# Weight sums of the projection behind the merge: made by accumulating DMAs in DRAM instead of by VectorE

## The chip, the cores and the metric

The kernel runs on one core of a Trainium2 chip. The metric is the device time of one execution in microseconds, the median of several runs. All inputs lie in the device's DRAM at the start, the output lies there at the end. The engines of the core are TensorE (PE in the profile), VectorE (DVE), ScalarE (ACT), GpSimd (POOL) and SyncE (SP); each works through its own queue in order, and waits for the others through semaphores. Transfers are issued from the queues of SP, ACT and POOL.

## The reference, cut to what matters

One layer of a streaming encoder: 512 frames, 1024 features, float32. After a norm, one projection gives q, k, v, the inputs of a recurrence and two gates; attention and recurrence are projected (`ya`, `yb`), gated and merged; the merge goes through `w_o`, and a gated feed-forward block follows.

```python
xn = rmsnorm(h, norm_mix_g[l])
u = jnp.einsum('bsd,de->bse', xn, w_in[l])
q, k, v, xr, gr, ga, gb = jnp.split(u, splits, axis=-1)
ya = chunked_band_attention(q, k, v, rel_table[l]) @ w_attn_out[l]
xc = causal_depthwise_conv(xr, conv_w[l], conv_b[l])
hr = rg_lru(xc, w_rg_r[l], b_rg_r[l], w_rg_i[l], b_rg_i[l], rg_lambda[l])
yb = (hr * jax.nn.gelu(gr)) @ w_rnn_out[l]
g_a, g_b = jnp.split(jax.nn.sigmoid(jnp.concatenate([ga, gb], axis=-1) + b_merge[l]), 2, axis=-1)
h = h + (g_a * ya + g_b * yb) @ w_o[l]
gu = rmsnorm(h, norm_ffn_g[l]) @ w_ffn_in[l]
g, up = jnp.split(gu, 2, axis=-1)
h = h + (jax.nn.silu(g) * up) @ w_ffn_out[l]
return rmsnorm(h, final_norm_g)
```

`w_o` is 1024x1024, `w_ffn_in` 1024x5632, `w_ffn_out` 2816x1024. The change concerns the product with `w_o`.

## The kernel before

**Products in parts.** Every weight tile is split into a high part in a reduced format (ScalarE, L86) and the rest (VectorE, L87), and every product is three matmuls, high by high, high by low, low by high (`mm3`, L78 to L82). A tile of weights for one product is two pieces of 128x1024; each goes from DRAM into one of three buffers tagged `raw`, is split into a buffer tagged `whl`, and frees the raw buffer with its split. `prefetch` and `weights` (L416 to L454) make the tiles in the order of a list of names, so many names ahead of the product that asks.

**Products in blocks.** The products of `v`, of `w_o` (called `o`) and most of the feed-forward input (units fg0, fu0, fg1, fu1, fg2, fu2) and output are made by Winograd's form of Strassen's scheme: both factors are cut into 2x2 blocks, and seven block products of sums take the place of eight. With weight blocks b11, b12, b21, b22 the sums are t1 to t4; the products are named w11, w21, t1, t2, w22, t3, t4. The sums of the left factor for `o` are made from the merged rows `ta` in the loop at L1174 to L1192.

**Where the sums of weights come from.** For `v` and the later units VectorE makes them next to the product. For `o` and for fg0 (called `f`) they are made early, in the loop of the recurrence, by `sums_kept` (L321): it loads four blocks of one half (u = 0 or 1) into the pool `obp`, makes the four sums (L327 to L330), stores them to DRAM, and for those in `kept_parts` splits them and stores both parts (L337 to L340). It is called at the end of loop steps j = 2, 4, 6 for (`o`, 0), (`o`, 1), (`f`, 0) and after the first tiles of q and k for (`f`, 1). `kept_weights` (L344) loads them back: t1 and t2 of `o` are split then, t3 and t4 come as parts, straight into weight tiles. The pool is closed after the last call, and `aw`, `aw2`, the pools of the attention, are opened on its place; their tiles wait for the last use of what lay there.

For the feed-forward output VectorE makes no sums: `out_copy` (L222) copies a block within DRAM through SP's queue, and `out_add` (L226) adds another block onto it by an accumulating DMA through POOL's queue. There are 16 copies and 16 adds of 512 KB. One copy goes with each head of the attention; four adds go in heads 9, 11, 13, 15, four with the loop at L1174, eight in units fg1 and fg2.

**The order.** The attention is a loop over 16 heads: transposes of the probabilities of head h, one piece of other projection work (`fill`), the scores of head h + 2, and the product with v; before it, while `yb` is projected, the sums of x for `v` (`x_sums`, L966) and the sums of v's weights. TensorE's order is written out by hand from the `v` products on. Elsewhere a planner orders each engine's instructions by priority and by simulated readiness; `keep_in_program_order` pins an instruction behind the one written before it on the same engine. So the first of each of the sums of x is pinned behind what VectorE has to do for the keys of the second pair, and the copies and adds are pinned in SP's and POOL's queues. In the `o` product the order is w11, w21, t1, t2, w22, t3, then the first half of the norm, with t4 (L1251) between its transposes, then fg0's w11.

## Time and profile before

| | |
|---|---|
| Time, median of 3 runs | 847.2 us (847.09 to 848.59) |
| The profiled execution | 848.82 us, span 847.0 us |
| PE busy | 837.2 us (99%) |
| DVE busy | 654.1 us (77%) |
| ACT busy | 524.3 us (62%) |
| POOL busy | 159.9 us (19%) |
| DMA | 153.96 MB, mean 182 GB/s |
| granted clock | 0.997 |

The busy time of PE counts a matmul from its start to its modelled end, and matmuls overlap: one of 512 columns is shown with some 0.39 us while the next starts 0.23 us after it. So a late matmul shows in the distance of starts, and only a longer stall as idle time. In rows of a group the columns are the line, the engine, the operation, out<-in, the count, and durations in ns; in rows of a timeline the start and the duration in us come first, and in brackets stands the idle time before the instruction with what ended it. In a table of stretches the columns are the stretch, its length, busy us of PE, PEld, DVE, ACT and POOL with their instructions, the granted clock, the DMA share and GB/s.

### The profile page before, as it was taken

Reading aid. Unit: us, or ns where it says so; the run is one execution under the profiler, and the core shown is the slowest. Engines: PE = TensorE matmul, PEld = TensorE weight load, DVE = VectorE, ACT = ScalarE, POOL = GpSimd, SP = SyncE. Lnnn points to the kernel's source line nnn. Section 1 sums busy time; section 2 is a strip of 40 time slices with the busy share of each in tenths; the row PEclk is TensorE's granted clock in tenths of the full one; section 3 lists DMA queues with packets and bytes.
Section 4 is the critical chain, followed back from the end, with each engine's and each line's share of the span. In section 5 each row is a group of like instructions: output and inputs, shape, how many; then the busy total and the mean of one; then the engine's idle time right before and its main releaser. Section 6 shows DMA issues by size and latency. Waiting matters only on the chain.

```text
span 847.0 us, 11664 instructions
## 1 busy us (share of the span) xinstructions
PE 837.2 (99%) x4102; PEld 708.8 (84%) x4102; DVE 654.1 (77%) x960; ACT 524.3 (62%) x868; POOL 159.9 (19%) x207
## 2 busy tenths in 40 slices
PE   9999999999999999999999999999999999999996
PEld 6988888888878888888888888888888999988885
DVE  6667779886999778777568777889777878599784
ACT  7595848773456678878544469663765466555543
POOL 2412030221040043343211000005102322200000
PEclk9999999999999999999999999999999999999998
DMA  8433386687565444549448984555955576455442
GB/s 286 166 103 117 130 298 243 212 271 243 167 205 150 132 134 148 157 152 223 94 132 211 320 294 154 157 187 166 229 176 159 150 187 207 140 177 168 160 165 99
DMA packets 104058, 153.96 MB, mean 182 GB/s; under 512 B 8024, under 2 KB 62896, under 8 KB 103488
## 3 DMA queue, kind: packets, MB, share of 16 engines
q1 hardware_dynamic: 99040, 141.32, 51.2%
q0 software_dynamic: 3728, 8.96, 6.4%
q10 hardware_dynamic: 1232, 2.95, 0.9%
q8 instruction: 32, 0.52, 0.3%
q14 instruction: 26, 0.21, 0.1%
HBM read 139.53 MB, written 30.45 MB: 201 GB/s over the span
## 4 chain that ended last, share of the span: by engine, by line
PE 84%; DVE 7%; ACT 4%; DMA 3%; issue 2%; ACTq 0%; DVEq 0%
PE fu_x L80 2%; PE fu_x L81 2%; PE fu_x L82 2%; PE o L1122 2%; PE fg_x L82 2%; PE fg_x L80 2%; PE fg_x L81 2%; PE pT L1102 2%; PE po_ga L82 2%; PE po_ya L80 2%; PE po_ya L82 2%; PE p_out L81 2%; PE p_out L80 2%; PE po_ya L81 2%; PE p_out L82 2%
## 5 line engine op out<-in xcount | busy, mean ns | idle before, releaser
L1326 POOL TENSOR_TENSOR sg<-sg,keep_fu_x 128x512 f32<-128x512 f32 (+1 forms) x10 | 17.8, 1784 | 163.4 <-DVE keep_fu_x L1325 163.4
L1091 POOL TENSOR_SCALAR p<-p,rl 128x128 f32<-128x128 f32 (+3 forms) x61 | 43.8, 733 | 13.7 <-DVE rl L1087 9.4
L1085 DVE CUSTOM_DVE_ANT_0 p<-s,bias 128x128 f32<-128x128 f32 (+1 forms) x64 | 28.6, 486 | 12.6 <-PE s L1077 11.1
L1086 ACT ACTIVATE p<-p,m 128x128 f32<-128x128 f32 (+1 forms) x64 | 35.5, 555 | 2.3 <-DVE m L1085 2.0
L87 DVE TENSOR_TENSOR whl_fu_w<-raw_fu_w,whl_fu_w 128x1024 fp32r<-128x1024 f32 (+1 forms) x18 | 22.1, 1230 | 9.0 <-ACT whl_fu_w L86 9.0
L87 DVE TENSOR_TENSOR pp<-pT,pp 128x384 fp32r<-128x384 f32 (+1 forms) x48 | 26.9, 595 | 2.0 <-ACT pp L86 1.8
L81 PE MATMUL po_xr<-xnT,whl_xr 128*128 128x512 f32 (+1 forms) x80 | 27.7, 354 | 0.0
L87 DVE TENSOR_TENSOR whl_fu_t<-t_fu,whl_fu_t 128x1024 fp32r<-128x1024 f32 (+1 forms) x18 | 23.2, 1293 | 5.9 <-ACT whl_fu_t L86 5.7
L81 PE MATMUL po_gr<-xnT,whl_gr 128*128 128x512 f32 (+1 forms) x80 | 27.5, 347 | 0.0
L82 PE MATMUL po_gr<-xnT,whl_gr 128*128 128x512 f32 (+1 forms) x80 | 27.3, 347 | 0.0
L82 PE MATMUL po_xr<-xnT,whl_xr 128*128 128x512 f32 (+1 forms) x80 | 27.3, 347 | 0.0
L80 PE MATMUL po_gr<-xnT,whl_gr 128*128 128x512 f32 (+1 forms) x80 | 27.2, 347 | 0.0
L738 POOL MEMSET bias<- 64x64 f32 x16 | 2.5, 155 | 130.7 <-DMA bias<-ext_d 130.7
L80 PE MATMUL po_xr<-xnT,whl_xr 128*128 128x512 f32 (+1 forms) x80 | 26.3, 352 | 0.4 <-ACT xnT L649 0.4
L86 ACT ACTIVATE whl_fu_w<-raw_fu_w 128x1024 fp32r<-128x1024 f32 (+1 forms) x18 | 17.7, 987 | 13.0 <-issue 7.1
L80 PE MATMUL po_k<-xnT,whl_qk 128*128 128x512 f32 x64 | 25.5, 398 | 0.0
L80 PE MATMUL po_q<-xnT,whl_qk 128*128 128x512 f32 x64 | 25.5, 398 | 0.0
L80 PE MATMUL po_ga<-xnT,whl_ga 128*128 128x512 f32 x64 | 25.5, 398 | 0.0
L80 PE MATMUL po_gb<-xnT,whl_gb 128*128 128x512 f32 x64 | 25.3, 395 | 0.0
L86 ACT ACTIVATE whl_fu_t<-t_fu 128x1024 fp32r<-128x1024 f32 (+1 forms) x18 | 17.7, 989 | 12.2 <-PE fu_x L82 8.9
L82 PE MATMUL po_ga<-xnT,whl_ga 128*128 128x512 f32 x64 | 25.1, 392 | 0.1
L81 PE MATMUL po_q<-xnT,whl_qk 128*128 128x512 f32 x64 | 25.0, 390 | 0.0
(610 smaller groups left out, 3036.8 us busy)
## 6 DMA issues: line engine op xcount, KB each, us to landing
raw_qk<-in_w_in_dram SPq DMA_DIRECT2D x32, 256.0 KB, 3.3
out_t<-in_w_ffn_out_dram SPq DMA_DIRECT2D x16, 512.0 KB, 5.5
raw_fu_w<-in_w_ffn_in_dram SPq DMA_DIRECT2D x16, 512.0 KB, 4.7
raw_fo<-in_w_ffn_out_dram SPq DMA_DIRECT2D x14, 512.0 KB, 4.3
raw_t<-out_t SPq DMA_DIRECT2D x24, 256.0 KB, 3.3
raw_xr<-in_w_in_dram SPq DMA_DIRECT2D x8, 512.0 KB, 6.0
raw_gr<-in_w_in_dram SPq DMA_DIRECT2D x8, 512.0 KB, 4.5
raw_ga<-in_w_in_dram SPq DMA_DIRECT2D x8, 512.0 KB, 4.9
```

The costliest lines, as they stand in the source:

```text
L80: pe.matmul(o, sh, mh, start=start, stop=False, skip_group_check=parts)
L81: pe.matmul(o, sh, ml, start=False, stop=False, skip_group_check=parts)
L82: pe.matmul(o, sl, mh, start=False, stop=stop, skip_group_check=parts)
L86: act.activation(hi, src, AF.Copy)
L87: dve.tensor_sub(lo, src, f(hi))
L738: pool.memset(b[64:128, 448:512], NEG)
L1085: dve.tensor_tensor_reduce(prob[qb][:], scs[qb][:, 0:w], bias[:, S - w:S], -1.0, 3e38, ALU.add, ALU.min, nmax[:, qb:qb + 1])
L1086: act.activation(prob[qb][:], prob[qb][:], AF.Exp, bias=nmax[:, qb:qb + 1], scale=-1.0, accum_out=lsum[:, qb:qb + 1])
L1091: eng.tensor_scalar(prob[qb][:], prob[qb][:], rl[:, qb:qb + 1], 1.0, ALU.mult, ALU.mult)
L1102: pe.transpose(pt[:, at * P:(at + 1) * P], prob[qb][:, kb * P:(kb + 1) * P], ident[:])
L1122: pe.matmul(po[:, S - n:S], st, pp[i][:, part, lo:lo + n], start=kb == 0 and part == 0, stop=kb == NT - 1 and part == 1)
L1326: (pool if keep and (unit != f_units[-1] or side) else dve).tensor_mul(o, o, keep[a] if keep else banks[a])
```

## The change

The four calls of `sums_kept` become two, (`f`, 0) and (`f`, 1), at j = 2 and j = 4. The sums of `o` are made in DRAM: in heads 0 to 7 of the attention SP copies a block into `o_t`, and in heads 2 to 9 POOL adds a block, or an earlier sum, onto it. Since such a DMA only adds, the signs change: t1 = b12 + b11, t2 = b22 + t1, t3 = b22 + b12, t4 = b21 + t2; the sums of the left factor take the opposite signs where needed (two additions and a subtraction at L1188 to L1190 become two subtractions and an addition), and two results go in with -0.5 in place of 0.5. All four sums of `o` are now loaded into raw buffers and split there, t3 and t4 too; the t3 product asks one name ahead instead of two. The subtractions of the splits of fg0's w11 are pinned in program order.

For the feed-forward output, eight copies stay in the attention, now in heads 8 to 15, and eight go into units fu0 and fg1; the first four adds go in heads 11, 13, 14, 15, the last eight in fu1 and fg2 (before fg1 and fg2). There the copies are pinned behind the weight loads written before them, one after each of the products w11, t1, t2 and w22.

```diff
--- before.py
+++ after.py
@@ -33,9 +33,10 @@
 CW = 256
 N_PLAIN = 3
 GROUP = 2
-COPIES = [1] * 16
-ADDS_AT = (9, 11, 13, 15)
-ADDS = {"fg1": 1, "fg2": 1}
+PINNED = (("f", "w11", 0), ("f", "w11", 1))
+COPIES = [0] * 8 + [1] * 8
+ADDS_AT = (11, 13, 14, 15)
+ADDS = {"fu1": 1, "fg2": 1}
 PAIR_TILES = 2 * (11 - N_PLAIN) - (4 - (N_PLAIN - 1))
 
 
@@ -311,8 +312,8 @@
             split(hl[u][:, 0], hl[u][:, 1], src)
         return lambda part, k: hl[k // 2][:, part, k % 2]
 
-    kept_sums = {(w, n): dr.tile([2, P, D], F32, name=f"{w}_t{n}") for w, n in (("o", 1), ("o", 2), ("f", 1), ("f", 2), ("f", 3))}
-    kept_parts = {(w, n): dr.tile([2, P, 2 * D], F32, name=f"{w}_hl{n}") for w, n in (("o", 3), ("o", 4), ("f", 4))}
+    kept_sums = {(w, n): dr.tile([2, P, D], F32, name=f"{w}_t{n}") for w, n in (("f", 1), ("f", 2), ("f", 3))}
+    kept_parts = {(w, n): dr.tile([2, P, 2 * D], F32, name=f"{w}_hl{n}") for w, n in (("f", 4),)}
 
     def kept_block(dst, w, kh, half, u):
         at = kh * S + u * CW
@@ -339,6 +340,24 @@
             for part, o in enumerate((hi, lo)):
                 sp.dma_start(out=kept_parts[w, n][u][:, part * D:(part + 1) * D], in_=f(o).rearrange("p k e -> p (k e)"))
 
+    o_t = {(kind, u): dr.tile([P, 2, S], F32, name=f"o_{kind}_{u}") for kind in ("t1", "t2", "t3", "t4") for u in range(2)}
+
+    def o_rows_of(kh, half, u):
+        at = kh * S + u * CW
+        return w_o[at:at + CW, half * S:half * S + S].rearrange("(k p) e -> p k e", p=P)
+
+    def o_copy(kind, u):
+
+        block = {"t1": (0, 1), "t2": (1, 1), "t3": (1, 1), "t4": (1, 0)}[kind]
+        tc.keep_in_program_order(sp.dma_start(out=o_t[kind, u][:], in_=o_rows_of(*block, u)))
+
+    def o_dma_add(kind, u):
+
+        two = o_rows_of(0, int(kind == "t3"), u) if kind in ("t1", "t3") else o_t["t1" if kind == "t2" else "t2", u][:]
+        tc.keep_in_program_order(pool.dma_start(out=o_t[kind, u][:], in_=two, accum_op=ALU.add, max_dma_last_dim=4096))
+
+    o_sums = [(kind, u) for kind in ("t1", "t2", "t3", "t4") for u in range(2)]
+    o_copies, o_adds = list(o_sums), list(o_sums)
     o_room = []
 
     def kept_weights(w, kind):
@@ -362,8 +381,11 @@
             if kind[0] == "w":
                 kept_block(raw[:], w, int(kind[1]) - 1, int(kind[2]) - 1, u)
             else:
-                sp.dma_start(out=raw[:].rearrange("p k e -> p (k e)"), in_=kept_sums[w, int(kind[1])][u])
-            split(hl[u][:, 0], hl[u][:, 1], raw[:])
+                sp.dma_start(out=raw[:], in_=o_t[kind, u][:] if w == "o" else kept_sums[w, int(kind[1])][u].rearrange("p (k e) -> p k e", k=2))
+            act.activation(hl[u][:, 0], raw[:], AF.Copy)
+            ins = dve.tensor_sub(hl[u][:, 1], raw[:], f(hl[u][:, 0]))
+            if (w, kind, u) in PINNED:
+                tc.keep_in_program_order(ins)
         return lambda part, k: hl[k // 2][:, part, k % 2]
 
     f_sums, f_loads, room = {}, [0], []
@@ -906,7 +928,8 @@
             if j == w == 0:
                 gates_of(j)
         if j:
-            sums_kept(obp, "oof"[j // 2 - 1], (0, 1, 0)[j // 2 - 1])
+            if j < 6:
+                sums_kept(obp, "f", j // 2 - 1)
 
     def blocks(ap):
         return ap.rearrange("p (b i) -> p b i", i=P)
@@ -950,7 +973,6 @@
 
     q_tile(0)
     k_tile(0)
-    sums_kept(obp, "f", 1)
     ob_stack.close()
     rw2_stack.close()
     rw_stack.close()
@@ -1158,8 +1180,12 @@
             if h + 2 < HEADS:
                 probs[h + 2] = scores(h + 2)
             weigh(h, pp)
+            if h < 8:
+                o_copy(*o_copies.pop(0))
             step(copies, COPIES[h])
-            if h in ADDS_AT:
+            if 2 <= h < 10:
+                o_dma_add(*o_adds.pop(0))
+            elif h in ADDS_AT:
                 step(adds)
     aw2_stack.close()
     aw_stack.close()
@@ -1185,9 +1211,9 @@
             split(msT[j][:, 0, high_], msT[j][:, 1, high_], s3[:])
         else:
             i = j - 4
-            dve.tensor_add(ta[j][:, high_], ta[i][:, high_], ta[j][:, high_])
+            dve.tensor_sub(ta[j][:, high_], ta[i][:, high_], ta[j][:, high_])
             dve.tensor_sub(ta[i][:, low_], ta[j][:, high_], ta[i][:, low_])
-            dve.tensor_sub(ta[j][:, low_], ta[j][:, low_], ta[i][:, low_])
+            dve.tensor_add(ta[j][:, low_], ta[j][:, low_], ta[i][:, low_])
             split_pair(msT[j], ta[j])
             split(msT[i][:, 0, low_], msT[i][:, 1, low_], ta[i][:, low_])
     z_stack.close()
@@ -1220,7 +1246,7 @@
     q2 = [cp.tile([P, 2], F32, name=f"hsq2_{t}") for t in range(NT)]
 
     def o_product(banks, kind, rows, start):
-        w = weights(f"o_{kind}", 2)
+        w = weights(f"o_{kind}", 1 if kind in ("t3",) else 2)
         src, kh, half = m_rows[rows]
         for a in range(2):
             toks = slice(half * 256 + a * P, half * 256 + (a + 1) * P)
@@ -1228,11 +1254,11 @@
                 mm3(banks[a][:], src[:, 4 * kh + k, 0, toks], src[:, 4 * kh + k, 1, toks], w(0, k), w(1, k),
                     start and k == 0, k == 3, parts=True)
 
-    def o_add(banks, half, cc, last=False):
+    def o_add(banks, half, cc, last=False, by=0.5):
         for a in range(2):
             t = 2 * half + a
             hs = ht[t][:, cc * S:(cc + 1) * S]
-            ins = dve.scalar_tensor_tensor(hs, banks[a][:], 0.5, hs, ALU.mult, ALU.add)
+            ins = dve.scalar_tensor_tensor(hs, banks[a][:], by, hs, ALU.mult, ALU.add)
             if half == a == cc == 0 and not last:
                 tc.keep_in_program_order(ins)
             if last:
@@ -1264,12 +1290,12 @@
     o_add(oz, 1, 1)
     tc.keep_in_program_order(act.activation(warm[:], eps_t[:], AF.Sqrt))
     o_product(ox, "t2", "s2", False)
-    o_add(ox, 0, 1)
+    o_add(ox, 0, 1, by=-0.5)
     o_product(oz, "w22", "s4", False)
     o_add(oz, 0, 1, True)
     o_rows(0)
     o_product(ox, "t3", "s3", False)
-    o_add(ox, 1, 1, True)
+    o_add(ox, 1, 1, True, by=-0.5)
     norm_half(x32p, ht, hsq, gf, hn_at, 0, "ffn", f_at, None, o_last_rows)
     ow_stack.close()
     ms_stack.close()
@@ -1417,6 +1443,8 @@
             actT[2 * i + c] = (hi[:, c], lo[:, c])
 
     def spare_work(kind):
+        if unit in f_units[1:3]:
+            step(copies, kind in after)
         if unit in ADDS and kind in after:
             step(adds, ADDS[unit], after=after[kind])
 
```

## The prediction

> **What bounds the kernel now.** I read the page first (busy time, the queues), then the waits of TensorE, then a table of stretches, the starts of single matmuls, and last the chain of waits with the order of each engine around the places where TensorE lost time.
>
> ```profile
> PE 837.2 (99%) x4102; PEld 708.8 (84%) x4102; DVE 654.1 (77%) x960; ACT 524.3 (62%) x868; POOL 159.9 (19%) x207
> ```
> ```profile
> PE v_z L81 <- DVE whl_v_t L87: 0.7, 1, 0.7
> ...
> PE s L1076 <- DVE m L1085: 0.2, 1, 0.2
> ```
> ```profile
> 97.00:142.00 45.00, 45.00 (x204) 36.73 (x204) 36.80 (x41) 30.93 (x41) 9.50 (x6) 1.00 0.73 261
> ```
>
> TensorE is the bound: 837.2 of 847.0 us of span. What a change of this kind can win is therefore not VectorE time but only the places where TensorE's matmuls start later than their turn. In 97 to 142 us, where both halves of the `o` sums are made, TensorE is busy 45.00 of 45.00 us. Taking work from VectorE there is worth nothing by itself.
>
> The losses that have to do with these sums lie later, between 217 and 255 us. The starts of the first matmul of each block show them (columns: start, duration, engine, line, operation):
>
> ```profile
> 217.64 0.22 PE L1076 MATMUL s<-kh,q 128*128 128x128 f32 x1
> ...
> 218.92 0.40 PE L80 MATMUL po_yb<-rnn,whl_yb 128*128 128x512 f32 x1
> ...
> 229.82 0.22 PE L1076 MATMUL s<-kh,q 128*128 128x128 f32 x1
> ...
> 231.59 0.40 PE L80 MATMUL po_yb<-rnn,whl_yb 128*128 128x512 f32 x1
> ...
> 242.50 0.39 PE L80 MATMUL v_x<-whl_v_w,xnT 128*128 128x512 f32 x1
> ...
> 248.56 0.39 PE L80 MATMUL v_z<-whl_v_t,v_s1h 128*128 128x512 f32 x1
> ...
> 255.04 0.39 PE L80 MATMUL v_x<-whl_v_t,v_s2h 128*128 128x512 f32 x1
> ...
> 260.48 0.39 PE L80 MATMUL v_z<-whl_v_w,v_s4h 128*128 128x512 f32 x1
> ```
>
> The first block of scores takes 218.92 - 217.64 = 1.28 us, the second, of the same eight matmuls, 1.77: 0.49 lost. A product of 24 matmuls without a stall takes 260.48 - 255.04 = 5.44 us; the first product of `v` takes 6.06 (0.62 lost), the second 6.48 (1.04 lost). Together 2.15 us. For the scores and the second product the waits name VectorE; I count the first product with them, since its weight splits come off the same queue. Why VectorE is late, the next rows show:
>
> ```profile
> 191.51 1.23 DVE L327 TENSOR_TENSOR f_b<-f_b,f_b 128x1024 f32<-128x1024 f32 x1
> ```
> ```profile
> 208.25 0.59 ACT L945 ACTIVATE kh<-po_k 64x512 fp32r<-64x512 f32 x1 [6.27 <-DMA f_hl<-f_b]
> ```
> ```profile
> 208.88 0.68 DVE L946 TENSOR_TENSOR kl<-po_k,kh 64x512 fp32r<-64x512 f32 x1 [4.63 <-ACT kh L945]
> ...
> 211.55 1.23 DVE L979 TENSOR_TENSOR v_s<-xnT 128x1024 f32<-128x1024 f32 x1
> ```
> ```profile
> 230.00:235.00 5.00, 4.77 (x23) 3.77 (x23) 5.00 (x9) 2.30 (x8) 0.00 (x0) 1.00 0.53 148
> 235.00:240.00 5.00, 5.00 (x23) 4.13 (x22) 5.00 (x6) 0.00 (x0) 3.54 (x3) 1.00 1.00 321
> ```
>
> The sums call for (`f`, 1), the last of the four, runs at 191.5 us. Its tiles lie where the attention's pool is opened next, so the copy of the second key tile `kh` waits 6.27 us for the last store `f_hl`, VectorE idles 4.63 us behind it, and the sums of x (`v_s`, L979), written behind those keys in program order, cannot begin before 211.55. By 230 us VectorE is busy 5.00 of 5 us, with no slack before the `v` products.
>
> **The change, part by part.** *The `o` sums leave the loop.* Per half four sums, two splits, four loads, two stores of sums and four of split parts go.
>
> ```profile
> L327 DVE TENSOR_TENSOR o_b<-o_b,o_b x2: 1211/1214/1218, 97.5 to 129.9; 128x1024 f32<-128x1024 f32 x2
> ```
>
> Twelve VectorE instructions at about 1.21 us are 14.6 us, all in the stretch that TensorE covers fully: 0 us.
>
> *The `f` sums move one and two places forward*, to where the `o` sums stood (97 and 130 us). Nothing is left at 191 to 208: six instructions at 1.23 us go (7.4 us), and with the store the waits of 6.27 and 4.63. The keys of the second pair can then be copied as soon as their product is done, and the sums of x start up to 10 us earlier. VectorE's lateness at the three places is about 1 us each (the largest loss is 1.04), far less than that. I take all three losses as gone: **-2.15 us**. The ends: nothing, if what is late there are the loads and weight buffers, and -2.15.
>
> *Eight copies and eight adds in the attention.* The copies take the place of copies of the output weights, one per head as before, on SP: no new wait. The adds are new on POOL, in heads 2 to 9.
>
> ```profile
> 310.31 0.34 SPq L737 DMA_DIRECT2D bias<-ext_d  x1
> ```
> ```profile
> 379.35 1.11 POOL L233 DMA_DIRECT2D out_t<-in_w_ffn_out_dram  x1
> ```
> ```profile
> 314.54 0.15 POOL L738 MEMSET bias<- 64x64 f32 x1 [6.91 <-DMA bias<-ext_d]
> ```
> ```profile
> 316.78 0.29 DVE L1085 CUSTOM_DVE_ANT_0 p<-s,bias 128x128 f32<-128x128 f32 x1 [0.96 <-PE s L1077]
> ```
>
> An add of the same size holds POOL 1.11 us. It stands behind the head's row scalings, and POOL idles 6.91 us before its next memset of the bias; a sum waits for a copy issued two heads before it. What comes next behind it, that memset, has 316.78 - 314.69 = 2.1 us before VectorE asks for it. Cost 0; if the cover goes, what the bias is later than 2.1 us.
>
> The Trainium skill (DMA: Bandwidth & Descriptors, "Issuing engines are not separate DMA queues") says that transfers started by any engine run on the same 16 DMA engines, interleaved. By it the adds on POOL's queue take time from the bias and weight loads of SP. The rows of heads 9 to 15 keep the sum at 845.1; the rule at its hardest gives the time of R3.
>
> *Eight copies of output weights move to fu0 and fg1, their adds to fu1 and fg2.* They wait for nothing; what they meet are the weight loads of these units.
>
> ```profile
> out_t<-in_w_ffn_out_dram SPq DMA_DIRECT2D x16, 512.0 KB, 5.5
> ```
> ```profile
> 554.54 1.50 SPq L380 DMA_DIRECT2D raw_fu_t<-in_w_ffn_in_dram  x2
> 561.06 2.17 SPq L380 DMA_DIRECT2D raw_fu_w<-in_w_ffn_in_dram  x2
> ```
> ```profile
> 568.48 1.22 DVE L87 TENSOR_TENSOR whl_fu_t<-raw_fu_t,whl_fu_t 128x1024 fp32r<-128x1024 f32 x1
> ```
> ```profile
> 570.70 0.39 PE L80 MATMUL fu_x<-whl_fu_t,bts 128*128 128x512 f32 x1
> ```
>
> The tightest: the second split of t3 stands behind a sum that waits for the second of these loads. It ends at 569.70; the product starts at 570.70 and reaches the second half six matmuls later (5.44 / 24 x 6 = 1.36): 2.36 us of slack. The last copy ahead of these loads stands behind the pair of 554.54, some 6 us earlier, and lands in 5.5. Cost 0; above, the 5.5 us of one whole copy less 2.36, 3.1 us; below, nothing, since no wait is taken away.
>
> *The `o` product splits t3 and t4 itself*: four more splits, and four loads of 512 KB through the raw buffers in place of four of 1 MB straight into the weight tiles. Two splits of f w11 are pinned behind the first subtractions of the norm.
>
> ```profile
> L86 ACT ACTIVATE whl_o_t<-raw_o_t x4: 1061/1062/1067, 465.9 to 475.5; 128x1024 fp32r<-128x1024 f32 x4
> L87 DVE TENSOR_TENSOR whl_o_t<-raw_o_t,whl_o_t x4: 1216/1218/1226, 467.0 to 479.1; 128x1024 fp32r<-128x1024 f32 x4
> ```
> ```profile
> 480.00:485.00 5.00, 5.00 (x24) 4.12 (x23) 2.80 (x5) 1.81 (x5) 0.00 (x0) 1.00 1.01 377
> 485.00:490.00 5.00, 5.00 (x24) 4.14 (x23) 3.56 (x4) 3.25 (x4) 0.00 (x0) 1.00 0.97 357
> 490.00:495.00 5.00, 5.00 (x24) 4.14 (x23) 1.54 (x3) 1.10 (x3) 0.00 (x0) 1.00 1.03 401
> 495.00:500.00 5.00, 5.00 (x24) 4.14 (x23) 4.39 (x8) 2.94 (x7) 0.00 (x0) 1.00 0.96 374
> ```
>
> Four splits are 4.9 us of VectorE and 4.2 of ScalarE. VectorE idles 20 - 12.29 = 7.7 us there and gets 2.4 more by the pin; ScalarE idles 10.9. The transfers, at a share of 0.96 to 1.03, become fewer: t3 and t4 are 2 MB in place of 4. Cost 0. What is close to the path is the hand-over to the norm:
>
> ```profile
> 496.75 0.68 DVE L1235 SCALAR_TENSOR_TENSOR h<-o_z,h 128x512 f32<-128x512 f32 x1
> ...
> 500.06 0.75 DVE L519 TENSOR_SCALAR xs_ffn<-h,rs_ffn 128x1024 f32<-128x1024 f32 x1
> ```
> ```profile
> 501.07 0.60 PE L532 MATMUL pt_ffn<-ident,xs_ffn 128*128 128x128 f32 x4
> ```
>
> The scaled rows end at 500.81, the transposes start at 501.07: 0.26 us of slack. Moving the f w11 splits out of this stretch gains some, a late t4 split would take it.
>
> **The sum** against the profiled execution: 848.82 us (span 847.0 and 1.8 around it) - 2.15 = 846.7. That execution lies 1.6 us over the median of the runs, 847.2; the same difference on the median gives **845.1 us** (0.25% less). A difference of 0.2%, 1.7 us, is about what a measurement of this kernel can tell from no change.
>
> **The rivals.** *R1, the stalls stay or go only in part.* For it: VectorE is not the only late party. The raw buffers and the weight buffers are freed by TensorE's own products, the last `yb` product holds two until 242.5, and the DMA share of 1.00 at 235 us is the loads of `v`. Against it: VectorE idled 4.63 us just before the backlog, and that wait goes. Half of the losses left gives 846.1, all of them 847.2.
>
> *R2, slower: a late raw load holds the hand-over to the norm.* t3, t4 and f w11 now pass through the same three raw buffers, each freed only by the split before. VectorE works in order; if the planner has put the last t4 split ahead of the `o_z` addition of 496.75, a late load holds that addition, the square, the root and both scalings behind it.
>
> ```profile
> whl_o_t<-o_hl SPq DMA_DIRECT2D x4, 1024.0 KB, 8.2
> ```
> ```profile
> 489.20 1.52 SPq L359 DMA_DIRECT2D whl_o_t<-o_hl  x2
> ```
>
> The second t4 load goes out at about 490.7 as now; with the 8.2 us of the row it lands at 498.9, its split (1.06 and 1.22) ends at 501.2, and the 4.06 us from 496.75 to 500.81 follow: transposes at 505.5, 4.4 us late. 845.1 + 4.4 = 849.5. It decides once the load lands after 494.5 (496.75 less the split), and makes the kernel measurably slower from 498.3 on. Against it: 8.2 us was for 1 MB at a full DMA share; half the bytes in a less loaded stretch should land in time.
>
> *R3, the adds make the attention's loads late* (the rule above). A bias that lands as late as those 1 MB loads, 8.2 us instead of the some 4.2 that pass before the memset, exceeds the 2.1 us of slack by 1.9 us, times eight heads 15 us: 860. Against it: the add at 379.35 lies among the same kind of loads, and TensorE lost nothing:
>
> ```profile
> 380.00:400.00 20.00, 20.00 (x112) 17.59 (x112) 16.21 (x41) 16.23 (x39) 7.12 (x13) 1.00 0.86 214
> ```
>
> *R4, the copies in fu0 and fg1 hold a split*: 845.1 + 3.1 = 848.2.
>
> **How the numbers follow.** The forecast 0.48, with a range of its own from 844.2 (0.9 below, for stalls at the hand-over to the norm that I didn't count) to 845.5 (0.4 of the losses left); R1 0.25; R2 0.14, a little over half of it at its full price, the rest at less; R3 0.05; R4 0.08, half of it with more than one product late. Faster: the forecast and the best of R1, 0.50. Slower: 0.08 of R2, R3, and 0.04 of R4, 0.17. The rest, 0.33, is no measurable change. The range from 844.0 to 849.0 holds the forecast, R1, the cheaper part of R2 and most of R4; it leaves out R3, the full price of R2 and a gain beyond 844.0, just under 0.2.
>
> **What would show it.** Right: no f_hl wait before `kh`; `v_s` L979 begins near 200 us; the first two `v` products take 5.44 us each; the transposes of the norm follow the t3 product at once. R1: 6 us and more for these products. R2: a gap of TensorE before `pt_ffn` released by `xs_ffn`. R3: TensorE idle in heads 2 to 9, a bias memset later than its scores. R4: idle in fu0 or fg1 released by a split of t3. The forecast is wrong if the span changes while the three places don't, or if they go and a new gap of over 1 us stands elsewhere.

## The result, and the profile after

The changed kernel takes 853.0 us at the median (850.2 to 859.3), the kernel before 847.9 in the same session (its first three runs, ahead of the prediction, had 847.2): a ratio of 1.0062, 95% interval 1.0037 to 1.0086. It is 0.6% slower; the forecast of 845.1 was wrong, and the range too. The profiled execution took 854.39 us (span 852.6), 5.57 more than that of before.

Line numbers move with the diff: the row scalings are L1113 (before L1091), the transposes of the probabilities L1124 (L1102), the memset of the bias L760 (L738), the first reduction of a head L1107 (L1085), the scaled rows L541 (L519), the transposes of the norm L554 (L532), the o additions L1261 (L1235), their squares L1266 (L1240), the splits of o and f w11 L385 and L386 (L86 and L87).

TensorE runs the same 4102 matmuls in the same order, so the start of each can be set against its start before. The difference grows or shrinks only where TensorE waits. This ledger, worked out from the two traces (us, by the time of before), holds for the changed kernel and, further down, for all experiments:

| stretch | 18 to 229 | v, 229 to 273 | heads, 273 to 479 | hand-over, 479 to 530 | fg0 to fg2, 530 to 730 | to the end |
|---|---|---|---|---|---|---|
| changed kernel | 0.00 | -2.17 | +4.13 | +2.00 | +1.43 | 0.00 |

With 0.36 from before 18 us that is 5.75 at the last matmul. This execution is the third longest of eleven, so its losses are more than the median run's. The gain came; three losses, each in work that the prediction had put at zero, are three and a half times as large.

**The gain.** The timeline of the changed kernel, first ScalarE and VectorE at the keys of the second pair, then the first matmul of each `v` product:

```profile
200.27 0.60 ACT L970 ACTIVATE kh<-po_k 64x512 fp32r<-64x512 f32 x1 [1.06 <-DVE kl L969]
```
```profile
200.26 1.23 DVE L1001 TENSOR_TENSOR v_s<-xnT 128x1024 f32<-128x1024 f32 x1
```
```profile
242.36 0.39 PE L81 MATMUL v_x<-whl_v_w,xnT 128*128 128x512 f32 x1
...
247.80 0.39 PE L81 MATMUL v_z<-whl_v_t,v_s1h 128*128 128x512 f32 x1
...
253.24 0.39 PE L81 MATMUL v_x<-whl_v_t,v_s2h 128*128 128x512 f32 x1
...
258.68 0.39 PE L81 MATMUL v_z<-whl_v_w,v_s4h 128*128 128x512 f32 x1
```

`kh` waits for no store any more, the sums of x begin at 200.26 in place of 211.55, and every product takes 5.44 us.

**The losses.** The waits of TensorE in the changed kernel (us in total, times, longest):

```profile
PE pT L1124 <- POOL p L1113: 2.0, 2, 1.8
PE pt_ffn L554 <- DVE xs_ffn L541: 1.5, 1, 1.5
...
PE fg_x L82 <- DVE whl_fg_w L88: 0.4, 1, 0.4
```

*In the heads* the long wait is in front of the transposes at 337 us. First POOL's queue around it, with a later head without the stall for comparison, then the bias load on SP's queue with VectorE, then TensorE:

```profile
325.67 1.07 POOL L357 DMA_DIRECT2D o_t<-in_w_o_dram  x1
333.33 0.14 POOL L760 MEMSET bias<- 64x64 f32 x1 [6.60 <-DMA bias<-ext_d]
333.58 3.56 POOL L1113 TENSOR_SCALAR p<-p,rl 128x128 f32<-128x128 f32 x4
...
372.71 2.05 POOL L1113 TENSOR_SCALAR p<-p,rl 128x128 f32<-128x128 f32 x4
```
```profile
326.64 0.34 SPq L759 DMA_DIRECT2D bias<-ext_d  x1
...
333.11 0.29 DVE L1107 CUSTOM_DVE_ANT_0 p<-s,bias 128x128 f32<-128x128 f32 x1 [0.96 <-PE s L1099]
...
335.36 1.21 DVE L88 TENSOR_TENSOR whl_qk<-raw_qk,whl_qk 128x1024 fp32r<-128x1024 f32 x1
```
```profile
334.85 0.52 PE L1124 MATMUL pT<-ident,p 128*128 128x128 f32 x3
337.19 1.70 PE L1124 MATMUL pT<-ident,p 128*128 128x128 f32 x7 [1.82 <-POOL p L1113]
...
339.54 0.63 PE L83 MATMUL po_q<-xnT,whl_qk 128*128 128x512 f32 x1
339.96 0.63 PE L81 MATMUL po_q<-xnT,whl_qk 128*128 128x512 f32 x1
...
341.25 0.40 PE L82 MATMUL po_q<-xnT,whl_qk 128*128 128x512 f32 x1
341.48 0.39 PE L83 MATMUL po_q<-xnT,whl_qk 128*128 128x512 f32 x1
```

The bias load goes out at 326.64, one us behind an add on POOL's queue (325.67), and POOL's memset waits for it until 333.33, 6.7 us in all. VectorE's reduction at 333.11 does not: it reads the bias of the head before. So the bias of this memset belongs to a head further on, while the four row scalings behind it in POOL's queue are those that the next transposes need. They come late, and the last of them runs into VectorE's weight split of 335.36: the four take 3.56 us where a later head without such an overlap takes 2.05. Three transposes run at 334.85; the fourth is the first to need the last scaled block, and it is the one that waits. Behind the stall the matmuls start 0.42 us apart in place of 0.23. The granted clock says why (a table of stretches of the changed kernel; after the length come busy us of PE, PEld, DVE, ACT and POOL, then the granted clock, DMA share, GB/s):

```profile
335.00:340.00 5.00, 3.17 (x15) 2.68 (x14) 4.42 (x9) 4.75 (x11) 4.18 (x5) 0.73 0.63 181
340.00:345.00 5.00, 5.00 (x22) 4.10 (x21) 1.13 (x2) 0.90 (x2) 3.41 (x6) 0.93 1.07 231
500.00:505.00 5.00, 3.96 (x19) 3.05 (x17) 1.89 (x6) 3.44 (x7) 0.00 (x0) 1.00 0.49 161
```

The clock lost is 5 x 0.27 + 5 x 0.07 = 1.7 us, so a wait of 1.8 costs 3.5 in all; by the starts of the matmuls it is 3.7 between 336 and 340 us.

*At the hand-over to the norm* (ScalarE, then VectorE, of the changed kernel):

```profile
497.34 1.06 ACT L385 ACTIVATE whl_o_t<-raw_o_t 128x1024 fp32r<-128x1024 f32 x1 [1.22 <-DMA raw_o_t<-o_t]
...
500.66 0.28 ACT L530 ACTIVATE sd_ffn<-hsq,eps_t 128x1 f32<-128x1 f32 x1
502.25 1.06 ACT L385 ACTIVATE whl_f_w<-raw_f_w 128x1024 fp32r<-128x1024 f32 x1 [1.32 <-DMA raw_f_w<-in_w_ffn_in_dram]
503.21 0.61 ACT L1266 ACTIVATE hj<-h 128x512 f32<-128x512 f32 x1
```
```profile
498.44 1.23 DVE L386 TENSOR_TENSOR whl_o_t<-raw_o_t,whl_o_t 128x1024 fp32r<-128x1024 f32 x1 [0.46 <-ACT whl_o_t L385]
...
499.64 0.68 DVE L1261 SCALAR_TENSOR_TENSOR h<-o_z,h 128x512 f32<-128x512 f32 x1
...
504.67 0.75 DVE L541 TENSOR_SCALAR xs_ffn<-h,rs_ffn 128x1024 f32<-128x1024 f32 x1
```

The t4 load lands at about 497.3, its split stands ahead of the `o_z` addition on VectorE, and then ScalarE's copy for f w11, in whose place the square `hj` could have run from 500.9 on, waits 1.32 us for its own load: `hj` runs at 503.21, the scaled rows end at 505.4. Of the 2.00 in the ledger 0.18 stand earlier, between 479 and 490 us; e1, which has nothing of this edit there, loses 0.40 at that place.

*From fu1 to fg2* POOL's products of fu1 run against VectorE's splits and sums for fg2:

```profile
666.63 1.94 POOL L1352 TENSOR_TENSOR sg<-sg,keep_fu_x 128x512 f32<-128x512 f32 x1 [1.77 <-DVE keep_fu_x L1351]
670.07 1.94 POOL L1352 TENSOR_TENSOR sg<-sg,keep_fu_x 128x512 f32<-128x512 f32 x1 [1.50 <-DVE keep_fu_x L1351]
```
```profile
666.48 0.94 DVE L88 TENSOR_TENSOR whl_fg_w<-raw_fg_w,whl_fg_w 128x768 fp32r<-128x768 f32 x1
667.34 2.04 DVE L408 TENSOR_TENSOR t_fg<-raw_fg_w,raw_fg_w 128x768 f32<-128x768 f32 x1
...
670.78 2.05 DVE L88 TENSOR_TENSOR whl_fg_w<-raw_fg_w,whl_fg_w 128x768 fp32r<-128x768 f32 x1
```

VectorE's instruction of 666.48, which starts ahead of POOL's product, takes 0.94 us; those that start while a product of POOL runs take 2.04 and 2.05 for the same shape. The Trainium skill (SBUF — State Buffer, "Who interferes with whom") says that a VectorE instruction with two inputs in SBUF contends with a GpSimd instruction that reads SBUF; these rows and the scalings at 333.58 agree with it.

### The profile page after: what moved, and what is told of

It reads as the page before. It is cut to its first block, busy times and chain, and to the rows that moved or that the text cites. A ratio compares the mean times of both kernels' runs of the same rounds, so it can differ in the third digit from the quotient of the medians.

```text
span 852.6 us, 11626 instructions
## 1 busy us (share of the span) xinstructions
PE 839.8 (99%) x4102; PEld 709.8 (83%) x4102; DVE 647.6 (76%) x952; ACT 524.2 (61%) x868; POOL 161.9 (19%) x215
## 3 DMA queue, kind: packets, MB, share of 16 engines
q1 hardware_dynamic: 97312, 132.93, 48.7%
## 4 chain that ended last, share of the span: by engine, by line
PE 86%; DMA 5%; DVE 4%; ACT 2%; issue 1%; POOL 0%; SPq 0%; ACTq 0%; DVEq 0%; POOLq 0%
PE fu_x L82 2%; PE fu_x L83 2%; PE fu_x L81 2%; PE pT L1124 2%; PE o L1144 2%; PE po_gb L81 2%; PE po_q L81 2%; PE po_xr L82 2%; PE po_xr L81 2%; PE po_q L82 2%; PE po_ga L83 2%; PE po_q L83 2%; PE po_ya L81 2%; PE po_ya L83 2%; PE po_gb L82 2%; PE po_yb L81 2%
## 5 line engine op out<-in xcount | busy, mean ns | idle before, releaser
L1107 DVE CUSTOM_DVE_ANT_0 p<-s,bias 128x128 f32<-128x128 f32 (+1 forms) x64 | 28.6, 485 | 17.4 <-PE s L1099 14.6
L1113 POOL TENSOR_SCALAR p<-p,rl 128x128 f32<-128x128 f32 (+3 forms) x61 | 37.4, 627 | 16.6 <-DVE rl L1109 12.3
L760 POOL MEMSET bias<- 64x64 f32 x16 | 2.3, 146 | 144.6 <-DMA bias<-ext_d 113.7
L88 DVE TENSOR_TENSOR whl_fu_t<-t_fu,whl_fu_t 128x1024 fp32r<-128x1024 f32 (+1 forms) x18 | 25.6, 1429 | 4.7 <-ACT whl_fu_t L87 4.6
L81 PE MATMUL po_q<-xnT,whl_qk 128*128 128x512 f32 x64 | 26.0, 406 | 0.0
L81 PE MATMUL po_ga<-xnT,whl_ga 128*128 128x512 f32 x64 | 25.4, 397 | 0.0
L82 PE MATMUL po_q<-xnT,whl_qk 128*128 128x512 f32 x64 | 25.4, 396 | 0.0
L87 ACT ACTIVATE whl_fu_w<-raw_fu_w 128x1024 fp32r<-128x1024 f32 (+1 forms) x18 | 17.7, 988 | 12.3 <-PE fu_z L83 7.4
L83 PE MATMUL po_q<-xnT,whl_qk 128*128 128x512 f32 x64 | 25.2, 393 | 0.0
L87 ACT ACTIVATE whl_fu_t<-t_fu 128x1024 fp32r<-128x1024 f32 (+1 forms) x18 | 17.7, 987 | 12.1 <-PE fu_x L83 9.8
```

The costliest lines, as they stand in the source:

```text
L81: pe.matmul(o, sh, mh, start=start, stop=False, skip_group_check=parts)
L82: pe.matmul(o, sh, ml, start=False, stop=False, skip_group_check=parts)
L83: pe.matmul(o, sl, mh, start=False, stop=stop, skip_group_check=parts)
L87: act.activation(hi, src, AF.Copy)
L88: dve.tensor_sub(lo, src, f(hi))
L760: pool.memset(b[64:128, 448:512], NEG)
```

## The experiments

The ledger of all kernels, made as above from one profiled execution each, beside the ratio of the times. The ratio and the ledger need not agree to a us, since one execution is not the median: the profiled ones of e4 and e5 are among the longest of their kernels, those of e2, e10 and e12 among the shortest. What a kernel costs is read from the ratio; the ledger says where.

| kernel | ratio (95% interval) | 18 to 229 | v | heads | hand-over | 530 to 730 |
|---|---|---|---|---|---|---|
| changed kernel | 1.0062 (1.0037 to 1.0086) | 0.00 | -2.17 | +4.13 | +2.00 | +1.43 |
| e1, sums two at j = 4 | 1.0056 (1.0036 to 1.0076) | +5.92 | -2.17 | 0.00 | +0.43 | -0.03 |
| e2, without the adds of o | 1.0017 (1.0000 to 1.0033) | +0.04 | -2.17 | 0.00 | +0.99 | +1.72 |
| e3, bias tiles kept | 1.0023 (1.0005 to 1.0041) | +0.05 | -2.17 | 0.00 | +1.19 | +2.22 |
| e4, ScalarE pinned | 1.0080 (1.0046 to 1.0114) | -0.01 | -2.17 | +7.80 | +1.87 | +3.10 |
| e5, adds in fg1 and fg2 | 1.0045 (1.0032 to 1.0058) | +0.05 | -2.17 | +6.90 | +1.37 | +1.33 |
| e6, memset behind | 1.0078 (1.0062 to 1.0095) | 0.00 | -2.17 | +6.77 | +0.67 | +1.22 |
| e7, e3 and e5 | 1.0004 (0.9991 to 1.0016) | +0.04 | -2.17 | 0.00 | +0.89 | +1.27 |
| e8, e3, e4 and e5 | 1.0000 (0.9990 to 1.0011) | -0.01 | -2.17 | 0.00 | +1.66 | +2.61 |
| e9, sums one step earlier | 0.9986 (0.9977 to 0.9994) | +0.04 | -2.17 | 0.00 | +0.11 | -0.01 |
| e10, o in the recurrence | 1.0029 (1.0016 to 1.0041) | +1.73 | -1.91 | 0.00 | +0.53 | +0.39 |
| e11, e10, own raw buffer | 1.0025 (1.0014 to 1.0035) | +2.08 | -2.05 | 0.00 | +0.40 | +0.74 |
| e12, copies for the adds | 1.0016 (1.0001 to 1.0032) | 0.00 | -2.17 | 0.00 | +0.44 | +1.98 |

**Where the gain comes from: e1 and e9.** Both are the kernel before, without any DMA add, with its VectorE sums moved.

```diff
-            sums_kept(obp, "oof"[j // 2 - 1], (0, 1, 0)[j // 2 - 1])
+            for w, u in {2: [("o", 0)], 4: [("o", 1), ("f", 0)], 6: [("f", 1)]}[j]:
+                sums_kept(obp, w, u)
...
-    sums_kept(obp, "f", 1)
```

> The kernel before, its VectorE sums of o and f kept, but all four of them inside the loop of the recurrence: (o, 0) at j = 2, (o, 1) and (f, 0) at j = 4, (f, 1) at j = 6, none after the keys. Nothing of the DMA adds is in it. Theory A (the stalls at 217 to 255 us come from the last sums standing at 191 us, as the prediction has it): kh no longer waits for f_hl, the two first v products take 5.44 us each, and the time is the kernel before less 2.1 us, about 845.8 beside 847.9 (ratio 0.9975). Rival B (the loads of v's weights and their buffers set these stalls, and the changed kernel gained there because the o sums' VectorE time left the loop): no gain, ratio 1.000, or a loss where two sums in one loop step make a product of the recurrence late.

853.7 us beside 848.5. The v products gained as theory A says, and the loop lost 5.9 us at one place. The waits of TensorE and the granted clock of e1:

```profile
PE rg L793 <- ACT xch L763: 3.7, 1, 3.7
```
```profile
165.00:170.00 5.00, 3.79 (x11) 2.64 (x12) 3.74 (x4) 4.94 (x8) 1.75 (x1) 0.66 0.94 286
```

Two calls in one step put the sums ahead of the convolution on VectorE (sums at 159.32 and 160.45, the convolution at 161.58), and a split of a sum, which waits 4.92 us for them, ahead of the copies on ScalarE: 3.7 us of waiting, and 5 x 0.34 = 1.7 of clock behind it. Part of B was right here, so the place had to be changed alone.

```diff
         if j:
-            sums_kept(obp, "oof"[j // 2 - 1], (0, 1, 0)[j // 2 - 1])
+            sums_kept(obp, "off"[j // 2 - 1], (1, 0, 1)[j // 2 - 1])
+        else:
+            sums_kept(obp, "o", 0)
...
-    sums_kept(obp, "f", 1)
```

> The kernel before, all its VectorE sums of o and f kept, each call one loop step earlier: (o, 0) at j = 0, (o, 1) at j = 2, (f, 0) at j = 4, (f, 1) at j = 6, none after the keys. Nothing of the DMA adds is in it. Theory A (the gain at the v products comes from the place of the last sums alone, and the kernel with two calls at j = 4 lost 5.5 us at 162 us because two calls crowd VectorE in one step): the v products take 5.44 us each, no product of the loop is late, 846 us, ratio 0.9975. Rival B (any sums moved earlier make the recurrence's convolutions late on VectorE): the gain is there, but as much or more is lost between 97 and 190 us, ratio 1.000 or more.

847.15 us beside 848.56, a ratio of 0.9986: faster than the kernel before by 1.4 us (0.5 to 2.0 by the interval), and so than the changed one. In the ledger nothing over 0.11 us but the -2.17 is left, in the v products, although all VectorE sums of o are still in the loop. The median gains somewhat less than the 0.9975 expected, which lies just outside the interval. Theory A holds: the gain is that of the place of the last sums, and has nothing to do with where the o sums are made.

**What stalls the heads: e2, e3, e6, e12.**

```diff
-            if 2 <= h < 10:
-                o_dma_add(*o_adds.pop(0))
-            elif h in ADDS_AT:
+            if h in ADDS_AT:
                 step(adds)
```

> The changed kernel without the eight adds of o in heads 2 to 9 (the sums of o are then only the copied blocks; the loads, splits and products of o are as they were, and so is the order of all engines but POOL). Theory A (the adds' traffic makes the bias loads land later, 5.7 us at the median where before had 4.1, and POOL's memset of the bias holds the row scalings behind it): the bias lands in about 4.1 to 4.5 us again, no idle time before the transposes in heads 3 to 12, and about 4 us go: 849 us, ratio 1.0015. Rival B (the copies on SP, or the order the planner gave, make the stall): the idle time before the transposes stays and so does the time, 853, ratio 1.006.

850.5 us, ratio 1.0017. The heads lose nothing, and some 0.45% of the time goes with the eight adds: theory A.

```diff
-        b = aw.tile([P, S], F32, tag="bias", bufs=2, name=f"bias{h}")
+        if h < 2:
+            biases.append(aw.tile([P, S], F32, tag=f"bias{h}", bufs=1, name=f"bias{h}"))
+            pool.memset(biases[h][64:128, 448:512], NEG)
+        b = biases[h % 2]
...
-        sp.dma_start(out=b[:], in_=band)
-        pool.memset(b[64:128, 448:512], NEG)
+        sp.dma_start(out=b[0:64, :], in_=band[0:64, :])
+        sp.dma_start(out=b[64:128, 0:448], in_=band[64:128, 0:448])
```

> The changed kernel with its adds, but two bias tiles are kept for all heads, their masked corner is set once, and the loads leave that corner out (two loads a head in place of one): POOL has no memset that waits for a load. Theory A (what stalls head 6 is POOL's in-order queue, the row scalings standing behind a memset that waits for the load of a later head's bias): the scalings start as soon as the row sums are there, the 2.0 us before the transposes and the slow matmuls behind them go although the bias lands as late as it did: 849 to 849.5 us, ratio 1.0015. Rival B (the late bias itself holds VectorE's first reduction of a head): TensorE still loses about 2 us in heads 3 to 9, now behind VectorE, 853. Rival C (a row scaling stretched by VectorE's work, 2.19 us in place of 0.69, is enough): one stall of 1 to 1.5 us stays, 851 to 852.

850.25 us, ratio 1.0023, and no loss in the heads with all adds in place: as A says, and against C. One thing was not as expected: the two half loads (3.6 and 4.5 us at the median) land earlier than the whole one did, so the kernel takes away part of the lateness too, not the order on POOL alone, and B was not tried. What speaks against B is the changed kernel itself: at the stall it is POOL, not VectorE, that waits for the load.

```diff
-        pool.memset(b[64:128, 448:512], NEG)
+        tc.keep_in_program_order(pool.memset(b[64:128, 448:512], NEG))
```

> The changed kernel with the memset of a head's bias kept in the written order on POOL: it stands behind the row scalings of the heads before, not ahead of them. Bias tiles, loads and adds are as in the changed kernel, so the loads land as late as there (median 5.7 us). The planner reorders VectorE and ScalarE within the attention for it. Theory A (the order on POOL's queue is what stalls head 6): no idle time of over 0.5 us before the transposes behind POOL's scalings, about 849.5 us, ratio 1.002, though the bias lands late. Rival B (the late landing itself is what counts, and the kernel with kept bias tiles gained because its two half loads land in 4.2 us): about 2 us of idle time stay in the attention, now behind VectorE's first reduction, ratio 1.006 or more.

855.2 us, ratio 1.0078: inconclusive. No transpose waits for POOL's scalings any more, which fits A. But the planner's new order makes the product of the next queries wait for VectorE in every second head, and the bias landed in 4.3 us at the median, with all eight adds in place, so neither theory was tried as meant:

```profile
PE po_q L81 <- DVE oacc L1146: 3.7, 5, 0.9
```

Is it the amount of traffic, or the kind? In e12 the same blocks go at the same places by plain copies on SP's queue.

```diff
-        tc.keep_in_program_order(pool.dma_start(out=o_t[kind, u][:], in_=two, accum_op=ALU.add, max_dma_last_dim=4096))
+        tc.keep_in_program_order(sp.dma_start(out=o_t[kind, u][:], in_=two))
```

> The changed kernel with the eight adds of o replaced, at the same places in heads 2 to 9, by plain copies of the same blocks issued on SP's queue (the sums of o then hold only the last block copied; all else, the order of TensorE, VectorE and ScalarE too, is that of the changed kernel). Theory A (it is the amount of traffic in these heads that makes the bias land late, by whichever queue it is issued): the bias still lands about 1.5 us later than in the kernel before, 5.5 us at the median, TensorE stalls before transposes behind POOL's scalings, 852 to 853 us, ratio 1.0045 to 1.006. Rival B (accumulating transfers on POOL's queue are what hurts, by the time they hold POOL and by what they take of the DMA engines beyond their bytes): the bias lands in about 4.2 us, no such stall, 849.5 us, ratio 1.0015 to 1.002, as without the adds.

849.8 us, ratio 1.0016, the heads lose nothing: rival B. The DMA issues of the bias (KB each, median us to landing) in before, the changed kernel and e12, in this order; then the same 10 us of the changed kernel and of e12; then the queues of the changed kernel, e2 and e12 (packets, MB, share of the 16 engines; the accumulating queue q0 of e12 has 6.3%, as in e2):

```profile
bias<-ext_d SPq DMA_DIRECT2D x16, 256.0 KB, 4.1
```
```profile
bias<-ext_d SPq DMA_DIRECT2D x16, 256.0 KB, 5.7
```
```profile
bias<-ext_d SPq DMA_DIRECT2D x16, 256.0 KB, 4.3
```
```profile
320.00:330.00 10.00, 10.00 (x56) 8.72 (x55) 8.66 (x22) 8.21 (x22) 2.55 (x5) 1.00 0.86 191
```
```profile
320.00:330.00 10.00, 10.00 (x56) 8.72 (x55) 8.47 (x21) 8.22 (x21) 2.19 (x5) 1.00 0.61 201
```
```profile
q1 hardware_dynamic: 97312, 132.93, 48.7%
q0 software_dynamic: 5392, 13.15, 9.5%
```
```profile
q1 hardware_dynamic: 97312, 132.93, 49.4%
q0 software_dynamic: 3728, 8.96, 6.3%
```
```profile
q1 hardware_dynamic: 98528, 137.12, 50.6%
```

With more GB/s (201 against 191) the copies keep the DMA engines less busy (0.61 against 0.86). Eight adds take 9.5 - 6.3 = 3.2% of the span, 27 us of all 16 engines, 3.4 us each; eight copies of the same 512 KB take 50.6 - 49.4 = 1.2%, 1.3 us each. The second is a rough figure, since the plain queue of kernels with the same traffic varies by 0.7% (48.7 in the changed kernel, 49.4 in e2). By single packets of the changed kernel's trace, those of 2048 bytes take 0.22 us at the mean on the accumulating queue and 0.10 on the plain one, those of 4096 bytes 0.37 and 0.18. An accumulating transfer takes the engines two to two and a half times as long per block. That the adds also hold POOL for some 1 us each (1.07 at 325.67) was not tried apart from it.

When the bias goes out counts as well. In the traces of the changed kernel, e4 and e5 the bias loads that go out 0.6 to 2.1 us behind an add of o land after 5.7 to 8.0 us. Those that go out ahead of one, or 3.5 us and more behind one, land after 3.5 to 4.7 up to 385 us, in e6 too, where all eight adds are in place. One in e6 that goes out 2.8 us behind takes 5.4. So a load is late when it goes out just behind an add. No run moved the adds alone against the loads.

**The hand-over and the feed-forward units: e4, e5, e7, e8.**

```diff
-            act.activation(hl[u][:, 0], raw[:], AF.Copy)
+            hi = act.activation(hl[u][:, 0], raw[:], AF.Copy)
+            if (w, kind, u) in PINNED:
+                tc.keep_in_program_order(hi)
```

> The changed kernel with ScalarE's copies of the two splits of f w11 pinned in program order, as VectorE's subtractions already are: they stand behind the squares of the last o addition. Theory A (the hand-over to the norm is late because these copies wait for their raw load ahead of the square hj on ScalarE): the 1.5 us before the second half of the first transposes of the norm go, 851.5 us, ratio 1.0043. Rival B (the t4 split or its load is what is late): the idle time before these transposes stays, ratio 1.006. Rival C (the copies pinned come too late for fg0's first product): the stall moves to that product, ratio 1.006 or more.

853.9 us, ratio 1.0080. The first transposes of the norm start on time, and 1.5 us go at those of 514 us (another 0.4 before 490): rival C's kind of outcome, though at the second transposes and not at the product. Its profiled execution has two stalls in the heads, at 336 and 377, each with 1.7 us of clock behind it (the wait of 1.8 us at 377, and the clock around it, in e4):

```profile
375.00:380.00 5.00, 3.19 (x15) 2.54 (x14) 4.45 (x9) 4.83 (x11) 4.12 (x5) 0.78 0.70 188
380.00:385.00 5.00, 5.00 (x22) 4.08 (x20) 0.97 (x2) 0.62 (x2) 3.28 (x5) 0.88 1.05 235
```

```diff
-ADDS = {"fu1": 1, "fg2": 1}
+ADDS = {"fg1": 1, "fg2": 1}
```

> The changed kernel with the last eight adds of the output weights back in fg1 and fg2, where before had them (the copies stay in fu0 and fg1). Theory A (in fu1 the adds, and the small copies that hold POOL until a tile is kept, push POOL's products of fu1 into the time of VectorE's sums and splits for fg2, which then take about 1.98 us in place of 1.2): the four small stalls of TensorE between 667 and 706 us, 1.2 us together in the changed kernel, go: its ratio falls by 0.0015 to about 1.005, and the offset of the last matmul against the one at 660 us is within 0.3 us. Rival B (the eight copies moved to fu0 and fg1 are what delays fg2): the stalls stay, ratio 1.006.

852.45 us, ratio 1.0045; its interval overlaps that of the changed kernel, so the time does not decide. In the traces the wait of `fg_x` for `whl_fg_w` at 667 us stands in all six kernels with adds in fu1 (the changed one, e2, e3, e4, e6, e12: 0.7 to 1.6 us by the starts of the matmuls) and in none of the five with them in fg1 (e5, e7, e8, e10, e11). But 1.33 us are lost in e5 all the same, at other products of fg2 and fu2, and up to 2.6 in e8. Where the copies too are back in the attention (e10, e11) 0.4 to 0.7 are left. So A is right for one stall, B seems to have a part in the rest, and the shares are not settled.

e7 and e8 put these edits together: e7 has the kept bias tiles and the adds in fg1 and fg2, e8 the pinned copies of ScalarE as well (the diffs above).

> The changed kernel with the kept bias tiles and the adds back in fg1 and fg2, both at once. Theory A (the losses stand in places of their own and add up): head 6 and the stretch from 667 us cost nothing, only the hand-over to the norm does (about 1 us); with the 2.0 us gained at the v products the time is about 0.7 us under the kernel before, ratio 0.999. Rival B (DMA traffic moved out of one place comes late at another): ratio 1.002 as with the kept bias tiles alone.

> As the kernel with the kept bias tiles and the adds in fg1 and fg2, and ScalarE's copies of the f w11 splits pinned behind the squares of the norm. Theory A (where the attention has no stall, the squares ahead of the copies take away the 1 us at the first transposes of the norm, and fg0's first product waits less than that): ratio 0.9975 to 0.9985. Rival B (the loss moves to the transposes at 514 us and fg0's first product, as it did where the copies alone were pinned, 1.3 us there): ratio 0.999 or more.

848.6 us, ratio 1.0004, and 848.5, ratio 1.0000: the level of the kernel before, not under it. For e7 that lies between its two theories. The loss in the heads and the stall at 667 are gone together, 1.0004 against 1.0023 with the bias tiles alone, though the two intervals overlap; 0.89 at the hand-over and 1.27 in the units eat the gain. For e8 it is rival B: 1.5 of its 1.66 us at the hand-over stand at 514 in place of 501.

**The o sums elsewhere: e10, e11.** In both, the same copies and adds of o stand in the loop of the recurrence, and the copies and adds of the output weights where before had them. The last two adds stand ahead of the copies of t4 there, so the product with t4 uses one block only; the transfers are the same.

```diff
-            if 2 <= h < 10:
-                o_dma_add(*o_adds.pop(0))
...
+            for _ in range(2 if j < 6 else 4):
+                o_dma_add(*o_adds.pop(0))
+        for _ in range(2):
+            o_copy(*o_copies.pop(0))
```

> The changed kernel, but the eight copies and eight adds of o stand in the loop of the recurrence (two copies a step from j = 0, two adds each at j = 2 and j = 4, four at j = 6), and the copies and adds of the output weights are where before had them. The order of TensorE, VectorE and ScalarE is that of the changed kernel to the last instruction; only SP's and POOL's queues differ. Theory A (the adds on POOL's queue and in the attention's traffic make the head stalls, and the moved copies and adds of the output weights the small stalls of fu1 to fg2): both go, the hand-over to the norm stays late by 1 to 1.5 us, and the gain of 2.1 us stays: 847.5 us, ratio 0.999. Rival B (the loop's loads of weights then come late, or the recurrence's work on POOL does): TensorE loses time between 97 and 216 us instead, ratio 1.002 or more. Rival C (the order given by the planner, not the queues, costs the time): stalls as in the changed kernel, 1.006.

850.5 us, ratio 1.0029. In its trace the heads lose nothing, the hand-over 0.5, the units 0.4: the order of the instructions on the computing engines, which is unchanged, was not the cause (C falls). But the loop pays, as B says. Its waits:

```profile
PE rg L815 <- POOL xch L786: 0.7, 1, 0.7
PE rg L815 <- ACT xch L785: 0.5, 1, 0.5
```

In e11 the two loads of t4 get a raw buffer of their own:

```diff
-            raw = wp.tile([P, 2, S], F32, tag="raw", bufs=3, name=f"raw_{w}_{kind}_{u}")
+            home, n = (o_room[0], 1) if (w, kind) == ("o", "t4") else (wp, 3)
+            raw = home.tile([P, 2, S], F32, tag="raw", bufs=n, name=f"raw_{w}_{kind}_{u}")
```

> As the kernel with the o sums in the loop of the recurrence, and the two loads of t4 go into a raw buffer of their own beside the weight buffers of o, in place of the three shared ones. Theory A (the splits of t3, t4 and f w11 come late to the hand-over since eight loads pass through three raw buffers, each freed by the split before it): t4 and f w11 land earlier, the squares and scaled rows are in time, and 1 to 1.5 us more go: 846.3 us, ratio 0.9975. Rival B (the order of the copies on ScalarE is what holds the squares, whenever the loads land): the idle time before the first transposes of the norm stays at 1 us or more, ratio 0.999.

850.1 us, ratio 1.0025; the hand-over loses 0.40 in place of 0.53. No difference that can be told. The loss expected there, 1 to 1.5 us, was not there in e10 either, so this says nothing on the changed kernel's 2.0.

## Why the prediction was wrong

**The gain was right, in place and size.** -2.15 us was the sum, from three places; -2.17 stands in the ledger, and e9 shows that it needs only the earlier place of the last sums. R1, the stalls stay, falls.

**"The o sums leave the loop: 0 us" was right.** e9 keeps them in the loop and gains the same.

**"The adds: cost 0" failed, and it is the largest error.** The step named the wrong waiter: it measured the slack of POOL's memset, 2.1 us, against VectorE's next reduction. That reduction reads the bias of another head (333.11 against the memset of 333.33, above). What stands behind the memset on POOL are the row scalings, and behind them the next transposes. Their slack could be read before, here SP, POOL and TensorE of the kernel before:

```profile
328.44 0.34 SPq L737 DMA_DIRECT2D bias<-ext_d  x1
```
```profile
314.78 2.97 POOL L1091 TENSOR_SCALAR p<-p,rl 128x128 f32<-128x128 f32 x4
...
331.65 0.15 POOL L738 MEMSET bias<- 64x64 f32 x1 [5.78 <-DMA bias<-ext_d]
331.89 3.11 POOL L1091 TENSOR_SCALAR p<-p,rl 128x128 f32<-128x128 f32 x4
```
```profile
318.51 1.28 PE L1102 MATMUL pT<-ident,p 128*128 128x128 f32 x10
...
336.65 1.28 PE L1102 MATMUL pT<-ident,p 128*128 128x128 f32 x10
```

Up to the first transpose that is 318.51 - 317.75 = 0.8 us and 336.65 - 335.00 = 1.7; up to the fourth, which needs the last block, 1.1 and 2.0. In the head that stalled the memset ran 331.65 - 328.44 = 3.2 us after the load went out before, and 6.7 in the changed kernel: 3.5 us later, where 2.0 were free, and the scalings took longer too. The median load, 1.6 us later, is past the smaller slack and within the larger. This was R3 in effect, at a chance of 0.05 and 15 us. Its size was off the other way: by the ratios of the changed kernel and e2 the adds cost about 0.45%, 3.8 us, since in the traces of the changed kernel and e4 only one or two heads stall for long, each for 3.6 to 4.1 us with the clock. The row that I set against R3, an add at 379.35 without harm, could show none: the next bias load went out at 382.84, 3.5 us behind it. And the price of an add stood in the page of before: its accumulating queue took 6.4% of the engines for 8.96 MB, the plain one 51.2% for 141.32, twice as much per MB.

**"The copies and adds of output weights: cost 0" failed.** 1.4 us are gone between 530 and 730 us. I looked for a late copy (R4) and did not ask what POOL does behind its new waits and adds in fu1: its products, which then run against VectorE's splits. R4's splits of t3 in fu0 and fg1 show no stall in the changed kernel.

**"The o splits of t3 and t4: cost 0" failed in the way of R2**, at 2.0 us in place of 4.4. Idle time of the two engines was enough, as the step said, but the order was not: the t4 split did stand ahead of the `o_z` addition. Its load landed at about 497.3, in the time of before 494.8 (TensorE was 2.5 late), 0.3 past R2's point of decision; the larger part came from what R2 did not have, ScalarE's copy of f w11 ahead of the square. The size is that of one execution: from 490 us on the changed kernel loses 1.8 here, and e2, e3, e6, e10 and e12, with the same instructions at this place, 0.5 to 1.0. What sets it is open.

**The chances.** Slower had 0.17, put together from rivals that were thought to exclude one another. They happened at once, and each was one of the zeros.

## What to carry to other kernels

For a wait that is made longer, follow the queue of the waiting engine, not the tile it waits for: behind the memset stood other work, with about half the slack (1.1 us against 2.1 at the tightest). An accumulating DMA is not a copy that also adds; price it from the queue table of the profile, by share per MB, and keep it away from small loads that an in-order queue waits for; here 3.5 us between the two were enough. And before a saving is bought with new work, ask which part of the edit makes it: here moving the calls of the sums one loop step earlier made the kernel faster than either version.

## What the runs showed of the hardware

- **A stall of TensorE of 1.8 us costs about twice its length.** After waits of 1.82 (changed kernel), 1.83 and 1.81 (e4), 1.61 (e5, with one of 0.34 behind it) and 3.7 us (e1), the granted clock lost 1.7 us each time, as the rows above add up for three of them. After 1.52 us at 505 it lost nothing (1.00), nor after the shorter waits of the other traces. The Trainium skill (TensorE: Matmul & The Clock Gate, "What's actually happening") says that the clock is halved after at least one idle window of about 3.4 us. 1.7 us lost at half rate are indeed 3.4 us; but here a wait of half a window, 1.6 us, was enough.
- **The changed kernel's times scatter over 9 us**, those of before over 4.7 in the same session. The executions that were profiled differ in how many heads stall, and where (337 here; 336 and 377 in e4; 394 and three short ones in e5), which would do it. That every longer execution has more stalls was not shown.
- **An accumulating transfer of 512 KB took all engines 3.4 us against some 1.3 for a copy**, and small loads that went out just behind one landed in 5.7 to 8.0 us in place of about 4. The Trainium skill (DMA: Bandwidth & Descriptors, "Issuing engines are not separate DMA queues") says that transfers run on the same 16 DMA engines whichever engine started them. The late loads on SP's queue beside adds from POOL's agree with it. The plain copies of e12, beside which the bias landed in 4.3 us, show that here the kind of the transfer decided.
